# Single PSUM banks, load orders and sums of squares in a hybrid attention block

## The chip, the cores and the metric

One Trainium2 chip, one of its cores. The metric is the device time of one execution in microseconds; the time of a kernel is the median of its runs. A profile comes from one execution that the hardware profiler recorded. Five engines work beside each other: TensorE (PE, matrix products), VectorE (DVE), ScalarE (ACT), GpSimd (POOL) and SyncE (SP). SP, ACT and POOL issue DMAs. Each engine takes its instructions strictly in order.

## The reference

One layer on a sequence of 1024 rows and 2048 columns, all in float32:

```python
hn = rmsnorm(h, norm_mix_g[i])
proj = hn @ w_in[i]                         # q, k, v, gate of two head groups
sb_out = stick_breaking_attention(...)      # 8 heads of 128
df_out = differential_attention(...)        # 8 heads, two softmaxes each
mixed = concatenate([sb_out * silu(sb_g), df_out * silu(df_g)])
h = h + mixed @ w_out[i]                    # the output projection
gate = sigmoid(rmsnorm(h, norm_ple_g[i]) @ w_ple_gate[i])
h = h + gate * (p[i] @ w_ple_proj[i])       # the embedding product
return rmsnorm(h, norm_final_g)
```

What follows is about the rows from the output projection on, and about the PSUM banks of the stage that makes values and gates.

## The kernel before

Everything is held transposed: 16 blocks of 128 columns of the model (the partitions) by two halves of 512 rows (the free size). One such block, 128x512 float32, is the unit of nearly every load and every vector instruction.

**Products.** A float32 product is made of three fast ones: operand and weight are each split into a rounded high part and a low rest, and high x high, high x low and low x high are added in PSUM. The high part is a copy on ScalarE, the low part a subtraction on VectorE. On top of that the kernel multiplies 2x2 block matrices with seven products instead of eight. The seven have the names A11, A12, S1, S2, S3, S4 and A22; weights are turned into differences first (`T1` to `T4` on VectorE, line 759, for the value stage and the projection; `second_diffs`, lines 1720 to 1724, for the gate, whose transformed weights S3 and A22 are stored in `tw_d` and loaded again by `last_load`, line 1702).

**Stages, in the order of time.** First values and gates (class `Seven`, object `gv`), then q, k and attention by heads, then the output projection (`Seven`, object `op`: first the products A11 and A12 of phase 0 for all blocks, then the loop over phase and block), then the gate stage: p1, p2 and gate1 for the products A11 and A12, p6, p5 and p3 for S2, S1 and S4, and the last stage for S3 and A22 (`begin` and the loop behind it) with the final norm.

**Order.** The orders of TensorE, VectorE and ScalarE are those of the text of the program. SP's and GpSimd's orders are made by a planner that simulates the program; `tc.issue_after(x)` puts an instruction behind x on its queue. `op.step()` is called after each product: it makes the high part (`whigh`, lines 792 and 794) and the low part (`wlow`, 806 and 808) of one weight that is needed some products later, then runs what is due in `op.soon`, then up to two or three operand splits out of `op.xq` (`split`, lines 679 to 687). So a ScalarE that waits for one late load holds every later cast back.

**Banks.** PSUM has eight banks of 128x512 float32. Pool `pp` has two tags, acc and t, with two banks each. Pool `pz` has two tiles of two banks each, for attention's scores; the other stages take one tile for a pair of sums b and c, or half of one.

**Squares.** After each block of the projection's second phase (32 blocks) and after each block of one half in the gate stage (16), ScalarE squares it and a GpSimd DMA adds it into a tile in DRAM, `sq_d`, two tiles for each of three sums. Before each norm the two tiles are loaded (`load_sums`) and one product with a matrix of ones for each adds over the partitions (`norm`, line 1931).

Of the kernel before, what the change touches and what calls it, by code (L numbers as in the profile page):

```python
# [70 lines left out]
def _body(ctx, nc, tc, ap):  # L71
# [552 lines left out]
    with tc.tile_pool(name="at", bufs=2) as at, tc.tile_pool(name="pz", bufs=2, space=PSUM) as pz:  # L624
# [363 lines left out]
        for _ in range(2):  # L988
            z = pz.tile([P, 2, HALF], F32, name="paz", tag="z")
            aa += [z[:, 0, :], z[:, 1, :]]  # L990
# [216 lines left out]
        for ph in range(2):  # L1207
            for u in range(2 * H):
# [117 lines left out]
        sq_d = dram.tile([3, 2, P, HALF], F32, name="sq_d", tag="sq_d")  # L1326
        SUMS = "S1", "S2", "S3", "S4"

        def load_operand(ph, nm, i, eng=nc.sync):
# [4 lines left out]
            if src is None:  # L1334
# [40 lines left out]
        nsq = [0, 0, 0, 0]  # L1375

        def add_squares(k, s):


            n = nsq[k]  # L1380
            nsq[k] += 1
            G.dma_start(sq_d[k, n % 2], s, **(dict(accum_op=ALU.add) if n > 1 else {}))
# [86 lines left out]

        for half in (1, 0):  # L1470
# [200 lines left out]
        op.ticks = True  # L1671
        gneg = ev.tile([P, NK], F32, name="gneg", tag="zm", bufs=1)
# [25 lines left out]
        def last_load(u, nm):  # L1698
            if u < 8:
                w = wp.tile([P, 2, 4 * P], F32, name="wraw", tag="wraw", bufs=2)  # L1700
                raws[u, nm] = [w[:, ks, :] for ks in range(2)]
                nc.sync.dma_start(w, tw_d[u, int(nm == "A22")])
# [4 lines left out]
        def second_hook(u, ks):  # L1707
            if (u, ks) == (6, 1):
# [9 lines left out]
        def second_diffs(u, ks):  # L1718
# [6 lines left out]
            if 1 <= u < 7:  # L1725
                for b in (12, 11, 22, 21):
                    second_load(u + 1, ks, b)
# [17 lines left out]
        for u in range(8):  # L1745
            for nm in ("S2", "S1", "S4"):
# [72 lines left out]
        def plew_load(u, c):  # L1819
            if u < 8:  # L1820
                pws[u, c] = ev.tile([P, 2, P], F32, name="pw", tag="sm", bufs=5)
                nc.sync.dma_start(pws[u, c], ap["w_pp"][u][:, :, c, :])
# [17 lines left out]
        for ph in range(2):  # L1840
            for u in range(8):
# [16 lines left out]
                elif ph == 1 and u == 7:  # L1858
                    b = pz.tile([P, 2, HALF], F32, name="pbc", tag="z")[:, 0, :]
                    c = None  # L1860
                else:
                    bc = pz.tile([P, 2, HALF], F32, name="pbc", tag="z")
                    b, c = bc[:, 0, :], bc[:, 1, :]
# [27 lines left out]
                if ph:  # L1891
                    V.tensor_tensor(u3, u3, r[0, u + 8], op=ALU.add)
                    if u == 7:
                        c = pz.tile([P, 2, HALF], F32, name="pbc", tag="z")[:, 1, :]
# [14 lines left out]
        gate_loads("A12", 4)  # L1909

# [15 lines left out]
        def norm(tiles):  # L1926

            out = tiles[0]
            ps = pp.tile([P, HALF], F32, name="ssps", tag="t")
            for i, t in enumerate(tiles):  # L1930
                T.matmul(ps, ones, t, start=i == 0, stop=i == len(tiles) - 1)
# [13 lines left out]

        def load_sums(half, tags):
            r = []
            for i, (pool, tag, n) in enumerate(tags):
                r.append(pool.tile([P, HALF], F32, name="sums", tag=tag, bufs=n))
                op.loaded = nc.sync.dma_start(r[i], sq_d[half, i])  # L1950
            return r
# [9 lines left out]
        def gating1(u, c, o, z):  # L1961
# [5 lines left out]
            def squared():  # L1967
                t = hc.pop(u + 8 * c)
                A.activation(o, t, AF.Square)
                A.dma_start(h_d[1, u + 8 * c], t)  # L1970
                add_squares(1, o)
# [6 lines left out]
        def p1(u):  # L1978
            if u % 4 > 1:
                pa[u] = pz.tile([P, 2, HALF], F32, name="paz", tag="z")[:, 0, :]  # L1980
# [19 lines left out]

        p1(0)
        p1(1)
        p1(2)
        op.calm = False
        embedding_load(1, "f")
        sums2 = load_sums(2, ((ev, "rstd1", 1), (ev, "ssq", 1)))
        p2(0)
        p2(1)
        norm(sums2)
        ssh[1] = sums2[0]  # L2010
        embedding(1)
        plew_load(0, 0)
        plew_load(1, 0)
# [3 lines left out]
        plew(0, 0)  # L2017
# [28 lines left out]
        def p6(u):  # L2046
# [8 lines left out]
            parts2[u] = pz.tile([P, 2, HALF], F32, name="pc", tag="z")[:, 0, :], w  # L2055
# [20 lines left out]
        for u in range(8):  # L2076
            p6(u + 1)
            plew_load(u + 2, 1)
            load_hc(u + 9)
            if u == 5:  # L2080
                sums0 = load_sums(0, ((ev, "rstd0", 1), (ev, "ssq", 1)))
# [7 lines left out]
            if u < 7:  # L2089
                plew(u + 1, 1)  # L2090
                p5(u + 1)
            if u == 6:
                norm(sums0)
                ssh[0] = sums0[0]
# [5 lines left out]
        def load_h(u):  # L2100
            if u < 8:
                hpair[u] = at.tile([P, 2, HALF], F32, name="h0", tag=HP[u], bufs=BUFS.get(HP[u], 2))
                nc.sync.dma_start(hpair[u], h_d[0].rearrange("(a k) p t -> k p a t", a=2)[u])

        def load_q(u):

            r = []
            for i in range(2):
                r.append(xp.tile([P, HALF], F32, name="qt", tag=f"x{'hl'[i]}{KT[4 + u % 4]}"))
                nc.sync.dma_start(r[i], q_d[u, i])  # L2110
# [5 lines left out]
        for u in range(4):  # L2116
            load_h(u)
        qs = {u: load_q(u) for u in range(3)}
# [14 lines left out]
        def final1(ch, u_):  # L2133
            t = ftile()
            nc.sync.dma_start(t, h_d[1, ch])

            def fn():
                V.scalar_tensor_tensor(t, t, gvec[:, 2, ch:ch + 1], sums1[0], op0=ALU.mult, op1=ALU.mult)
# [261 lines left out]
```

## Time and profile before

| | us |
|---|---|
| median of 3 runs (2388.27 to 2389.63) | 2388.85 |
| the profiled execution | 2393.9 |
| its span, first to last instruction | 2392.1 |
| TensorE busy | 2332.3 |
| VectorE busy | 1781.2 |
| ScalarE busy | 1189.3 |
| GpSimd busy | 334.3 |

The span is what the profile sees; the execution lasts 1.8 us longer. A row of waits reads: the engine, the tile and line that waited, what it waited for, the microseconds in total, how often, the longest one. A row of a group reads: line, engine, operation, output and inputs, shapes and count, then busy time, mean nanoseconds of one, the idle time of the engine before them and what ended it. L1897 is line 1897 of the kernel before.

### The profile page before, as it was taken

Reading aid. Unit: us, or ns where it says so; the run is one execution under the profiler, and the core shown is the slowest. Engines: PE = TensorE matmul, PEld = TensorE weight load, DVE = VectorE, ACT = ScalarE, POOL = GpSimd, SP = SyncE. Lnnn points to the kernel's source line nnn. Section 1 sums busy time; section 2 is a strip of 40 time slices with the busy share of each in tenths; the row PEclk is TensorE's granted clock in tenths of the full one; section 3 lists DMA queues with packets and bytes.
Section 4 is the critical chain, followed back from the end, with each engine's and each line's share of the span. In section 5 each row is a group of like instructions: output and inputs, shape, how many; then the busy total and the mean of one; then the engine's idle time right before and its main releaser. Section 6 shows DMA issues by size and latency. Waiting matters only on the chain.

```text
span 2392.1 us, 32521 instructions
## 1 busy us (share of the span) xinstructions
PE 2332.3 (97%) x11102; PEld 1936.5 (81%) x11102; DVE 1781.2 (74%) x3107; ACT 1189.3 (50%) x2213; POOL 334.3 (14%) x497
## 2 busy tenths in 40 slices
PE   9999999999999999999999999999999999999997
PEld 7878878888788877887888888888878777778776
DVE  7489776666577787777888867768778886677687
ACT  6334243333366675445677764545634334533453
POOL 1211112323200000000011101101111231011000
PEclk9999999999999999999999999999999999999998
DMA  7798589999977788777656666668888899998955
GB/s 253 244 345 285 162 242 286 287 280 273 294 248 253 242 276 279 258 252 249 208 169 199 179 211 206 196 197 256 208 205 228 255 265 293 294 330 280 317 189 179
DMA packets 257510, 590.46 MB, mean 247 GB/s; under 512 B 29056, under 2 KB 41344, under 8 KB 257344
## 3 DMA queue, kind: packets, MB, share of 16 engines
q1 hardware_dynamic: 178384, 395.15, 48.8%
q0 software_dynamic: 59664, 158.10, 26.0%
q10 hardware_dynamic: 19296, 35.14, 4.3%
q8 instruction: 87, 1.43, 0.3%
q14 instruction: 79, 0.65, 0.1%
HBM read 374.37 MB, written 222.30 MB: 249 GB/s over the span
## 4 chain that ended last, share of the span: by engine, by line
PE 72%; DVE 11%; DMA 8%; ACT 7%; issue 2%; SPq 0%; ACTq 0%; DVEq 0%
PE acc L262 7%; PE acc L264 7%; PE acc L263 7%; PE pbc L703 6%; PE pbc L705 6%; PE pbc L704 6%; PE pa L705 2%; PE pa L704 2%; PE pa L703 2%; PE tp L481 2%; DMA wraw<-w_gate 1%; DMA wraw<-w_out 1%; PE pb L1918 1%; PE pb L704 1%; PE pb L705 1%
## 5 line engine op out<-in xcount | busy, mean ns | idle before, releaser
L794 ACT CAST wpr<-T 128x512 fp32r<-128x512 f32 x208 | 125.5, 620 | 442.9 <-DVE T L759 359.4
L262 PE MATMUL acc<-xh,whi 128*128 128x512 f32 x768 | 315.1, 410 | 0.0
L264 PE MATMUL acc<-xh,wlo 128*128 128x512 f32 x768 | 302.3, 394 | 1.1 <-DMA wlo<-wlo_d 1.1
L263 PE MATMUL acc<-xl,whi 128*128 128x512 f32 x768 | 301.0, 392 | 0.0
L264 PEld LDWEIGHTS acc<-xh,wlo 128*128 128x128 f32 x768 | 144.4, 188 | 35.0 <-DMA wlo<-wlo_d 2.3
L263 PEld LDWEIGHTS acc<-xl,whi 128*128 128x128 f32 x768 | 145.5, 189 | 24.0
L262 PEld LDWEIGHTS acc<-xh,whi 128*128 128x128 f32 x768 | 145.0, 189 | 23.8 <-DVE qk L1549 0.4
L794 ACT CAST wpr<-wraw 128x512 fp32r<-128x512 f32 x144 | 88.3, 616 | 148.3 <-DMA wraw<-w_gate 36.8
L808 DVE TENSOR_TENSOR wpr<-T,wpr 128x512 fp32r<-128x512 f32 x208 | 142.8, 686 | 13.1 <-ACT wpr L794 9.2
L927 POOL DMA_DIRECT2D vg_d<-hc x120 | 86.8, 724 | 344.1 <-DVE hc L1169 206.7
L808 DVE TENSOR_TENSOR wpr<-wraw,wpr 128x512 fp32r<-128x512 f32 x144 | 97.9, 686 | 38.6 <-ACT wpr L794 38.5
L504 DVE TENSOR_TENSOR awl<-tp,awh 128x256 fp32r<-128x256 f32 (+1 forms) x160 | 92.5, 578 | 43.0 <-ACT awh L499 42.2
L499 ACT CAST awh<-tp 128x256 fp32r<-128x256 f32 (+1 forms) x160 | 80.6, 503 | 82.6 <-PE tp L481 76.4
L322 DVE CUSTOM_DVE_ANT_0 z<-z,masks 128x512 f32<-128x512 f32 (+7 forms) x128 | 97.1, 769 | 22.9 <-PE z L342 13.8
L703 PE MATMUL pbc<-cS,wpr 128*128 128x512 f32 x288 | 112.2, 389 | 0.8 <-DVE u L1225 0.8
L705 PE MATMUL pbc<-cS,wpr 128*128 128x512 f32 x288 | 112.1, 389 | 0.0
L704 PE MATMUL pbc<-cS,wpr 128*128 128x512 f32 x288 | 112.0, 389 | 0.0
L374 DVE TENSOR_TENSOR_SCAN st<-pt 128x511 f32<-128x511 f32 (+3 forms) x64 | 86.7, 1354 | 27.5 <-ACT pt L367 27.0
L367 ACT ACTIVATE pt<-z 128x512 f32<-128x512 f32 (+3 forms) x64 | 41.8, 653 | 76.9 <-DVE z L350 74.9
L529 PE MATMUL av<-awl,v 128*128 128x256 f32 x256 | 73.5, 287 | 2.0 <-DVE awl L504 2.0
L527 PE MATMUL av<-awh,v 128*128 128x256 f32 x256 | 72.0, 281 | 0.7 <-ACT awh L499 0.7
L528 PE MATMUL av<-awh,v 128*128 128x256 f32 x256 | 72.2, 282 | 0.0
(570 smaller groups left out, 6831.8 us busy)
## 6 DMA issues: line engine op xcount, KB each, us to landing
wlo<-wlo_d SPq DMA_DIRECT2D x94, 512.0 KB, 5.1
whi<-whi_d SPq DMA_DIRECT2D x74, 512.0 KB, 4.0
wraw<-w_vg SPq DMA_DIRECT2D x130, 256.0 KB, 4.6
vg_d<-hc POOLq DMA_DIRECT2D x120, 256.0 KB, 5.5
wraw<-w_in SPq DMA_DIRECT2D x54, 512.0 KB, 5.3
wraw<-w_gate SPq DMA_DIRECT2D x92, 256.0 KB, 5.4
wraw<-w_out SPq DMA_DIRECT2D x72, 256.0 KB, 4.8
wlo_d<-wlo SPq DMA_DIRECT2D x34, 512.0 KB, 3.4
```

The lines of the kernel that those rows point to most:

```text
L262: T.matmul(acc[c], hi[:, k2, kh, c, :], xh, start=first, stop=False)
L263: T.matmul(acc[c], hi[:, k2, kh, c, :], xl, start=False, stop=False)
L264: T.matmul(acc[c], lo[:, k2, kh, c, :], xh, start=False, stop=last)
L322: V.tensor_tensor_reduce(z, z, mwide[:, 0:n], -DF_SCALE, 3.0e38, ALU.add, ALU.min, mx)
L374: V.tensor_tensor_scan(st[:, off + 1:nkey], pt[:, off:nkey - 1], pt[:, off:nkey - 1], initial=1.0, op0=ALU.mult, op1=ALU.bypass)
L504: V.tensor_tensor(wl[:, o, :], tp[:, o, :], wh[:, o, :].bitcast(F32), op=ALU.subtract)
L703: T.matmul(o, wh[:, w], xh, start=start and k == 0, stop=False, skip_group_check=True)
L704: T.matmul(o, wh[:, w], xl, start=False, stop=False, skip_group_check=True)
L705: T.matmul(o, wl[:, w], xh, start=False, stop=k == 3, skip_group_check=True)
L794: A.copy(t[:, 0], src)
L808: V.tensor_tensor(t[:, 1], src, t[:, 0].bitcast(F32), op=ALU.subtract)
L927: G.dma_start(vg_d[hf, blk, u], o, **(dict(accum_op=ALU.add) if ph else {}))
```

## The change

Five things change together.

- Banks: outside attention the four banks of `pz` become four single tiles, `single(name)`. The pool is closed and opened anew around attention.
- Sums of squares: `sq_d` is gone. For the projection's 32 blocks ScalarE squares into one scratch tile (the mask's memory, `spare32`) and GpSimd adds it into a total in SBUF. For the 16 blocks of the gate stage VectorE adds into that scratch tile. A norm takes one tile.
- Places and times of the gate's operands (`GPLACE`, `NEXT`, `GNEXT`): A11, A12, S1, S4 and A22 take other buffers; three of A12's last four are loaded earlier.
- The gate's order: S2 and S1 of blocks 0 and 1 come before S4 of both, in the weights and in the products (`p5(1)` before `p3(0)`); one weight block of block 2 is loaded in S4's hook.
- Loads that follow others: the embedding's weights, `h`, `q` and the final loads are issued behind `op.loaded`, which the loads of transformed weights now set; fewer of them are loaded in advance. The embedding's first weights are cast earlier.

```diff
+    with tc.tile_pool(name="at", bufs=2) as at, ExitStack() as banks:
+        def singles(name):
+            banks.close()
+            pool = banks.enter_context(tc.tile_pool(name=name, bufs=4, space=PSUM))
+            return lambda nm: pool.tile([P, HALF], F32, name=nm, tag="z")
+
+        single = singles("pv")
...
-                    bc = pz.tile([P, 2, HALF], F32, name="pbc", tag="z")
-                    b, c = bc[:, 0, :], bc[:, 1, :]
+                    b, c = single("pbc"), single("pbc")
...
-        GPLACE = {"A11": XP[0:4] + FREE1, "A12": XP[4:12], "S2": FREE2 + [("at", t) for t in ("k", "k2", "v2", "v")],
-                  "S1": XP[12:16] + FREE1, "S4": XP[4:12], "S3": XP[0:4] + FREE2, "A22": XP[12:16] + XP[8:12]}
-
-        NEXT = {"A11": [("A11", 0)], "S3": [("A11", 4, 3)], "S1": [("A11", 7, 1), ("A12", 0)]}
+        GPLACE = {"A11": XP[0:4] + XP[8:12], "A12": XP[4:8] + FREE1, "S2": FREE2 + [("at", t) for t in ("k", "k2", "v2", "v")],
+                  "S1": XP[12:16] + XP[8:12], "S4": XP[4:8] + FREE1, "S3": XP[0:4] + FREE2, "A22": XP[12:16] + XP[8:12]}
+
+        NEXT = {"A11": [("A11", 0)], "S2": [("A11", 4, 3)], "S3": [("A11", 7, 1)], "S1": [("A12", 4, 3), ("A12", 0)]}
         GNEXT = {("A11", 1): [("S1", 4)], ("A12", 0): [("S4", 0)], ("A12", 1): [("S4", 4)],
-                 ("S2", 1): [("S3", 4)], ("S1", 1): [("A22", 0)], ("S4", 1): [("A22", 4)]}
+                 ("S2", 1): [("S3", 4)], ("S1", 1): [("A22", 0), ("A22", 4)]}
...
-        def add_squares(k, s):
-            n = nsq[k]
-            nsq[k] += 1
-            G.dma_start(sq_d[k, n % 2], s, **(dict(accum_op=ALU.add) if n > 1 else {}))
+        spare32 = masks.bitcast(F32)[:, 0:HALF]
+        totals = {}
 
         def row_squares(hf, o):
-            n = nsq[3]
-            nsq[3] += 1
-            t = ev.tile([P, HALF], F32, name="rsq", tag=f"rstd{n % 2}", bufs=1)
-            A.activation(t, o, AF.Square)
-            add_squares(2 * hf, t)
+            if hf not in totals:
+                totals[hf] = ev.tile([P, HALF], F32, name="total", tag=f"rstd{hf}", bufs=1)
+                A.activation(totals[hf], o, AF.Square)
+            else:
+                A.activation(spare32, o, AF.Square)
+                G.tensor_tensor(totals[hf], totals[hf], spare32, op=ALU.add)
...
         def second_hook(u, ks):
+            if u == 0:
+                second_load(2, ks, 22)
...
-        for u in range(8):
-            for nm in ("S2", "S1", "S4"):
+        for u, nms in [(0, ("S2", "S1")), (1, ("S2", "S1")), (0, ("S4",)), (1, ("S4",))] + [(u, ("S2", "S1", "S4")) for u in range(2, 8)]:
+            for nm in nms:
...
-                nc.sync.dma_start(pws[u, c], ap["w_pp"][u][:, :, c, :])
+                with tc.issue_after(op.loaded.ins):
+                    nc.sync.dma_start(pws[u, c], ap["w_pp"][u][:, :, c, :])
...
-        gate_loads("A12", 4)
+        gate_loads("A12", 7, 1)
...
             def squared():
                 t = hc.pop(u + 8 * c)
-                A.activation(o, t, AF.Square)
+                if u + c == 0:
+                    A.activation(spare32, t, AF.Square)
+                else:
+                    A.activation(o, t, AF.Square)
+                    V.tensor_tensor(spare32, spare32, o, op=ALU.add)
                 A.dma_start(h_d[1, u + 8 * c], t)
-                add_squares(1, o)
...
         p5(0)
         for u in range(8):
             p6(u + 1)
+            if u == 0:
+                p5(1)
...
-        for u in range(4):
+        for u in range(2):
             load_h(u)
-        qs = {u: load_q(u) for u in range(3)}
+        qs = {u: load_q(u) for u in range(2)}
```

`last_load` keeps its DMA as `op.loaded`; `load_h`, `load_q` and `final1` issue theirs behind it.

More of the change, by code (lines that the diff above doesn't have):

```diff
@@ L987, in _body @@
         aa = [pp.tile([P, HALF], F32, name="pa", tag=t, bufs=2) for t in ("acc", "acc", "t", "t")]
-        for _ in range(2):
-            z = pz.tile([P, 2, HALF], F32, name="paz", tag="z")
-            aa += [z[:, 0, :], z[:, 1, :]]
+        aa += [single("paz") for _ in range(4)]
         def outer(n):
@@ L1701, in last_load @@
                 raws[u, nm] = [w[:, ks, :] for ks in range(2)]
-                nc.sync.dma_start(w, tw_d[u, int(nm == "A22")])
+                op.loaded = nc.sync.dma_start(w, tw_d[u, int(nm == "A22")])
         def second_load(u, ks, b):
@@ L1893, in _body @@
                     if u == 7:
-                        c = pz.tile([P, 2, HALF], F32, name="pbc", tag="z")[:, 1, :]
+                        c = single("pbc")
                         prod(u, ph, "S1", c, True)
@@ L1924, in gprod, with norm @@
                 op.step()
-        def norm(tiles):
-            out = tiles[0]
+        def norm(out):
             ps = pp.tile([P, HALF], F32, name="ssps", tag="t")
-            for i, t in enumerate(tiles):
-                T.matmul(ps, ones, t, start=i == 0, stop=i == len(tiles) - 1)
+            T.matmul(ps, ones, out, start=True, stop=True)
             def roots():
@@ L2016, in _body @@
         load_hc(1)
-        plew(0, 0)
         gate_loads("S2", 0, eng=A)
@@ L2109, in load_q @@
                 r.append(xp.tile([P, HALF], F32, name="qt", tag=f"x{'hl'[i]}{KT[4 + u % 4]}"))
-                nc.sync.dma_start(r[i], q_d[u, i])
+                with tc.issue_after(op.loaded.ins):
+                    nc.sync.dma_start(r[i], q_d[u, i])
             return r
@@ L2214, in _body @@
         W = {(u, nm, ks): op.wq.pop((u, "g" + nm, ks)) for u in (6, 7) for nm in ("S3", "A22") for ks in range(2)}
-        z = {u: pz.tile([P, 2, HALF], F32, name="ple", tag="z") for u in (6, 7)}
+        z = {(u, c): single("ple") for u in (6, 7) for c in range(2)}
         Q = HALF // 2
```

74 lines of the change are left out of this document (33 added, 41 removed).

## The prediction

> **What bounds the kernel now.** I read the page's first part, then TensorE's busy time by stretches, then the waits of TensorE, then the queues around each wait.
>
> ```profile
> span 2392.1 us, 32521 instructions
> PE 2332.3 (97%) x11102; PEld 1936.5 (81%) x11102; DVE 1781.2 (74%) x3107; ACT 1189.3 (50%) x2213; POOL 334.3 (14%) x497
> ```
>
> TensorE sets the time; no edit here takes a product away, so gain must come out of its stalls. Busy time understates them (a matmul lasts 0.39 us but the next starts sooner), so I count matmuls in stretches of one shape (columns: stretch and length; busy us and count of TensorE, its weight loads, DVE, ACT, POOL; granted clock; DMA share; GB/s):
>
> ```profile
> 1750.00:1836.00 86.00, 86.00 (x382) 71.19 (x381) 64.50 (x102) 26.57 (x47) 16.27 (x19) 1.00 0.86 214
> 1733.80:1746.00 12.20, 7.72 (x26) 5.59 (x25) 7.67 (x12) 3.33 (x6) 0.85 (x1) 0.86 0.57 144
> 1855.00:1978.00 123.00, 120.63 (x527) 98.17 (x526) 99.59 (x154) 45.54 (x82) 34.02 (x50) 1.00 0.93 261
> 1997.60:2028.70 31.10, 29.52 (x125) 23.01 (x124) 18.13 (x28) 16.30 (x28) 3.72 (x5) 1.00 0.89 275
> 2028.70:2051.00 22.30, 19.24 (x82) 14.82 (x81) 12.50 (x21) 10.96 (x18) 0.00 (x0) 1.00 0.88 301
> 2100.00:2134.00 34.00, 29.48 (x114) 23.14 (x113) 27.26 (x46) 15.20 (x28) 4.28 (x6) 0.90 1.00 339
> 2246.00:2257.00 11.00, 9.76 (x40) 7.13 (x39) 8.53 (x14) 8.24 (x14) 1.45 (x2) 1.00 1.03 375
> 2257.00:2287.00 30.00, 27.99 (x123) 22.54 (x122) 23.82 (x41) 15.76 (x29) 0.87 (x1) 1.00 0.93 314
> 2287.00:2343.00 56.00, 56.00 (x245) 45.70 (x244) 45.79 (x76) 30.77 (x54) 0.00 (x0) 1.00 0.58 196
> ...
> 60.00:630.00 570.00, 564.47 (x2476) 465.15 (x2475) 398.45 (x597) 211.85 (x347) 135.58 (x209) 1.00 0.88 270
> ```
>
> The first row is a stretch without a stall. A window also counts the matmul cut by its edge, some 1.7 of them, so the pace is 86 / 380.3 = 0.227 us, and a product of 12 takes 2.72 us. Length less 0.227 x (count less 1.7) is what a window lost, to about 0.3 us in a short one; the four passes of a norm (three windows) are taken out of the count and stay in the loss. In order: 6.7, 3.8, 4.0, 4.1, 8.5, 3.2, 2.5 and 1.7 us, 34.5 from the output projection on; and some 8 us in the value and gate stage, the last row. The granted clock of 0.86 and 0.90 in two of them says that a long stall is paid again in slow matmuls after it. The eighth window has no stall, only a norm, so a norm's four passes cost 1.7 us.
>
> Whom TensorE waited for:
>
> ```profile
> PE pbc L703 <- ACT wpr L794: 4.5, 1, 4.5
> PE z L1836 <- ACT pwhl L1828: 3.6, 2, 2.2
> PE pbc L703 <- DVE hc L1247: 3.5, 2, 2.5
> ...
> PE pbc L703 <- DVE hq L1897: 2.3, 3, 0.9
> ...
> PE pb L1920 <- DVE wpr L808: 1.9, 1, 1.9
> ...
> PE pc L1918 <- DVE hc L2061: 1.7, 2, 1.2
> ...
> PE pa L1918 <- DVE o L1996: 1.6, 1, 1.6
> ...
> PE pbc L703 <- DVE hc L1169: 1.3, 2, 0.8
> ```
>
> **The change part by part.**
>
> *Banks.* A product that adds into half of a two-bank tile waits for readers of both halves. In the projection, A22 adds into b, which L1890 reads; TensorE waits for L1897, which reads c:
>
> ```profile
> 1895.53 0.69 DVE L1890 TENSOR_TENSOR u<-pbc,s 128x512 f32<-128x512 f32 x1
> ...
> 1896.98 0.69 DVE L1897 TENSOR_TENSOR hq<-pbc,u 128x512 f32<-128x512 f32 x1
> ```
>
> With a bank of its own, b is free 1.45 us earlier (1896.98 less 1895.53), more than the longest wait, 0.9: the 3.8 us of the window from 1855 go if DVE is no later than now. In the value stage the same edit drops one instruction of about 0.7 us from both L1247 waits and all of the two L1169 waits: 0.7 + 0.7 + 1.3 = 2.7 us of the 8; nothing if DVE falls as far back again, 5 if the slow clock after the 2.5 us wait goes too. I take 2.7. Reopening the pools adds no instruction; if it adds a wait, that shows at the projection's first product into a new bank. For L1996, p1(4) no longer takes the bank that gate1(0) still reads.
>
> *Order of loads at the projection's start.* DVE stood 4.72 us for a block of w_out, while five loads of w_pp, not needed for 300 us, went out on SP's queue around it:
>
> ```profile
> 1721.09 1.28 SPq L1822 DMA_DIRECT2D pw<-w_pp  x2
> ...
> 1723.07 0.55 SPq L1822 DMA_DIRECT2D pw<-w_pp  x1
> 1723.71 0.78 SPq L750 DMA_DIRECT2D wraw<-w_out  x1
> 1724.53 1.25 SPq L1822 DMA_DIRECT2D pw<-w_pp  x2
> pw<-w_pp SPq DMA_DIRECT2D x32, 128.0 KB, 4.7
> 1736.66 0.69 DVE L759 TENSOR_TENSOR T<-wraw 128x512 f32<-128x512 f32 x1 [4.72 <-DMA wraw<-w_out]
> ```
>
> Held behind the gate's first operands, they leave. Five loads of a median 4.7 us are about what DVE lacked. I take 6.5 of 6.7; nothing if GpSimd's three adds into comb_d in the same microseconds are the cause.
>
> *Squares: 48 DMAs that add up in DRAM, and six loads of the sums, go.*
>
> ```profile
> L1382 POOL DMA_DIRECT2D sq_d<-rsq x32: 542/868/1212, 1854.7 to 2010.5; - x32
> L1382 POOL DMA_DIRECT2D sq_d<-o x16: 552/879/929, 2058.1 to 2275.0; - x16
> L934 POOL MEMSET wide<- x1: 526/526/526, 0.9 to 0.9; 128x512 f32 x1
> q0 software_dynamic: 7056, 17.04, 46.8%
> L1965 DVE TENSOR_TENSOR hc<-hc,o 128x512 f32<-128x512 f32 x16 | 11.1, 692 | 0.6
> L1969 ACT ACTIVATE o<-hc 128x512 f32<-128x512 f32 x16 | 10.1, 630 | 8.8 <-DVE hc L1965 8.8
> ```
>
> The q0 row (packets, MB, share of the DMA engines) is of 1850 to 2015: 17.04 MB are 65 GpSimd DMAs of 128x512 f32 (0.262 MB); they held 46.8% of 165 us, 1.19 us each, so the 32 there free 38 us of DMA time, 23% of a stretch whose share is 0.89 to 0.93, and the 16 later ones 19 us. In their place come 30 GpSimd adds of 128x512, and 15 DVE adds in the gate stage. No row has a GpSimd add. Below stands the memset of that shape, 0.53 us for one stream; two inputs and an output, one after another, give 1.6. I take the middle, 1.1. GpSimd has room (34 of 123 us), and with one scratch tile ScalarE's next square waits for the add: at most one square in a product's 2.72 us, and 0.63 (L1969's squares) + 1.6 = 2.2 fits; behind it on ScalarE would stand the next weight cast.
>
> What can cost is DVE. If an add keeps DVE standing for g us, all of its length or a part, 24 fall into the window from 1855 (30 x 123 / 156), where DVE is idle 23.4 us: 0.98 us each, and beyond it DVE sets the pace. Below that an add in the burst before L1890 still eats the banks' 1.45. I leave 1.8 of the 3.8 us; the ends are 3.8 gained and, at 1.6 us, 24 x 0.62 = 15 lost.
>
> The Trainium skill speaks against this edit: SBUF — State Buffer, "Who interferes with whom", lets a VectorE instruction with two SBUF inputs and a GpSimd one that reads SBUF exclude each other for a whole instruction, and GPSIMD Engine Reference, "Elementwise — side-by-side cycle accounting", has 4497 ns for an add of 2048 elements, an estimate of 1.12 us for 512. By both the sum would be some 5 us smaller (24 x 0.14, and the 1.8). No row here shows it: there is no GpSimd add in this trace.
>
> *Norms.* One sum tile instead of two halves 1.7 us, three times. At 2247 TensorE waits for L2061 right behind the norm, so that one is worth nothing: 2 x 0.85 = 1.7.
>
> *Start of the gate.*
>
> ```profile
> 2019.82 0.72 ACT L681 ACTIVATE cgA12h<-cgA12l,gvec 128x512 fp32r<-128x512 f32 x1 [2.74 <-DMA cgA12l<-h_d]
> 2041.18 0.40 ACT L1828 CAST pwhl<-pw 128x256 fp32r<-128x256 f32 x1 [0.40 <-ACT s L1985]
> L794 ACT CAST wpr<-wraw 128x512 fp32r<-128x512 f32 x96 | 58.7, 614 | 103.3 <-DMA wraw<-w_gate 36.8 <-DMA wraw<-tw_d 34.0 <-DMA wraw<-w_out 23.9
> ```
>
> Three of the last four A12 loads now go out one product earlier, and 23% less stands before the fourth: 2.3 us (4.0 less the norm), none if it still lands late. The cast at 2041.18 moves ahead of the norm's work, and the bank of L1996 is free: I take 3.5 of 4.1.
>
> *Order of S2, S1, S4 (window 2100 to 2134).* S2 of block 1 is made two weights earlier, and S4's first use comes one product pair (5.4 us) later, past its late loads. The first half of the loss, the cast for the eighth embedding product, waits for S1's operands, helped only by lighter traffic. 5.5 of 8.5; ends 2 and 8.5.
>
> *Last stage.*
>
> ```profile
> 2247.01 2.74 SPq L2103 DMA_DIRECT2D h<-h_d  x4
> ...
> 2252.60 3.54 SPq L2110 DMA_DIRECT2D qt<-q_d  x3
> qt<-q_d SPq DMA_DIRECT2D x16, 256.0 KB, 5.0
> ```
>
> The h and q loads go ahead of the transformed weights that ScalarE waits for (34.0 us above); now they follow those. 2.0 of 2.5, ends 0 and 2.5. The loss at 2246 stays.
>
> *New waits.* Each DVE add is 0.69 us plus a wait of up to 0.63 for its square, behind it the next low weight half; 15 make 20 us where DVE is about 80% busy (27.26 of 34), so mostly covered. At L808 and L2061 TensorE waited for DVE three times; 3 x 0.69 = 2. The q loads come with one block less lead: 2 more. Ends 0 and 9.
>
> Sum: 2.7 + 6.5 + 1.8 + 1.7 + 2.3 + 3.5 + 5.5 + 2.0 = 26.0, less 4 = 22.0. The profiled execution took 2393.9 us (span 2392.1 and 1.8 around it), 5 above the median: 2371.9 against it, 2366.9 against the median of 2388.85.
>
> **The rivals.**
> 1. *Adds stop DVE* (place: 1853 to 2010). For: DVE is the busiest engine after TensorE there, and most of its instructions read two SBUF tiles. Against: 23.4 us of idle DVE. Mild, g = 1.2: 24 x 0.22 = 5.3 and the 1.8 more, 2374. Slower than before only from g = 0.98 + 20.2 / 24 = 1.82 us on, with nothing left of the 1.8; at 2.2 us it is 24 x 1.22 less 20.2 = 9.1 over, 2398. That lies beyond my upper bound of 1.6.
> 2. *Loads stay the bound*: the waits for w_gate come back once TensorE is earlier. Half of the gate's 13.3 us is lost: 2373.6. For: shares of 0.88 to 1.00; against: 57 us of DMA time less.
> 3. *Held loads come too late* in the last stage. A q load lands in 5.0 us, and S3 covers 5.4; 2 us late in six blocks is 10 us: 2377.
> 4. *Everything goes* but the 2246 loss and the untouched part of the value stage: 2.7 + 6.7 + 3.8 + 1.7 + 2.3 + 4.1 + 8.5 + 2.5 = 32.3, 2356.5.
>
> **How the numbers follow.** Forecast 45% (2362 to 2372); mild form of 1 13%, its slow form 6%; 2 14%; 3 10%; 4 12%. About 0.2%, 4.8 us, can be told from no change. The range, 2356 to 2384, reaches from 4 to 2 and 3 together. Slower 0.08 (the slow form and a late load in the tail), within 0.2% 0.07 (two of the rivals at once), faster 0.85.
>
> **What would show it.** Right: no DVE wait for w_out near 1731 and a clock of 1.00 there; no TensorE wait for L1897's successor; a GpSimd add near 1.1 us; DMA share near 0.70 from 1850 to 2000; norms of two passes; no waits for the embedding's weights at 2041. Wrong: DVE instructions of over 0.7 us beside adds, ScalarE waiting for GpSimd, waits for q or h loads after 2260, or the w_out wait still there.

## The result and the profile after

| | before | after |
|---|---|---|
| median, us (4 runs each) | 2388.56 (2388.14 to 2389.63) | 2366.27 (2361.72 to 2369.79) |
| profiled execution, us | 2393.9 | 2369.79 |
| TensorE busy, us | 2332.3 | 2321.1 |
| VectorE busy, us | 1781.2 | 1809.0 |

The ratio is 0.9908, with a 95% interval from 0.9893 to 0.9924. 2366.9 was forecast. The total agrees to 0.6 us; several of its terms do not, and their errors cancel, so that agreement is luck. The two profiled executions differ by 24.1 us.

The first lines of the page of the changed kernel:

```profile
span 2368.0 us, 32422 instructions
PE 2321.1 (98%) x11096; PEld 1932.0 (82%) x11096; DVE 1809.0 (76%) x3122; ACT 1189.4 (50%) x2213; POOL 336.0 (14%) x479
```

TensorE's busy time by stretches, columns as in the prediction (stretch and length; busy us and count of TensorE, weight loads, VectorE, ScalarE, GpSimd; clock; DMA share; GB/s):

```profile
1724.00:1737.00 13.00, 11.16 (x40) 8.12 (x39) 10.31 (x17) 4.47 (x8) 1.28 (x2) 0.87 0.67 156
1847.00:1970.00 123.00, 120.89 (x528) 98.50 (x527) 114.90 (x152) 44.60 (x79) 45.88 (x48) 1.00 0.62 209
1970.00:1993.70 23.70, 21.71 (x89) 17.45 (x89) 21.88 (x29) 15.28 (x26) 11.50 (x12) 0.93 0.82 282
1993.70:2021.00 27.30, 27.30 (x122) 22.62 (x121) 18.93 (x28) 13.55 (x24) 2.18 (x3) 1.00 0.82 280
2021.00:2043.00 22.00, 22.00 (x97) 17.87 (x96) 13.10 (x22) 12.68 (x21) 0.00 (x0) 1.00 0.75 245
2092.00:2126.00 34.00, 34.00 (x151) 28.16 (x150) 32.40 (x54) 15.14 (x29) 2.18 (x4) 1.00 0.90 313
2222.00:2233.00 11.00, 10.95 (x47) 8.47 (x46) 10.11 (x17) 8.94 (x14) 0.54 (x1) 1.00 0.86 283
2233.00:2262.00 29.00, 29.00 (x129) 24.02 (x129) 25.36 (x43) 17.20 (x32) 0.00 (x0) 1.00 0.71 246
...
60.00:630.00 570.00, 565.62 (x2487) 465.95 (x2485) 399.32 (x602) 213.05 (x351) 135.61 (x209) 1.00 0.88 271
```

With the prediction's measure (length less 0.2267 us for each matmul but 1.7) the rows from 1993.70 on lost next to nothing beyond a norm's two passes: the gate's stalls are gone, all of them. The first three rows still lose 4.3, 3.7 and 3.9 us. There are two places: the stall near 1731 is still there, only shorter, and the projection's second phase, 1847 to 1993.7, now loses 7.6 us, where the same work before lost 3.8. It became slower. The rows of waits name what TensorE waited for:

```profile
PE pbc L709 <- DVE u L1893: 4.1, 6, 2.0
...
PE pbc L709 <- DVE u L1248: 3.1, 3, 1.7
...
PE pbc L709 <- ACT wpr L800: 1.8, 1, 1.8
...
PE pbq L2228 <- DVE qt L2235: 1.3, 1, 1.3
PE pb L709 <- DVE u L1248: 1.3, 2, 0.9
```

The first is the second phase: L1893 is the read of b that L1890 was before. The edit to the banks did what it says, TensorE now waits for the reader of b and no longer for that of c; but that reader is late. The fourth is new and lies in the tail.

Since matmuls come in the same order in all these kernels, each stage can be timed from the start of its first matmul to that of the next stage's. This table is worked out so, in us, with the least time that the stage's matmuls take at 0.2267 us (norms not counted):

```
                        v and g  attention  projection 1  projection 2  gate A11,A12  S2,S1,S4  S3,A22   tail
matmuls x 0.2267                               108.8         152.3          97.9        141.5     81.6
before                   666.65   1056.51      116.75        156.28        109.82       149.55    85.93   30.54
after                    663.77   1054.54      113.99        159.83         98.82       142.60    82.51   32.15
gain                       2.9       2.0          2.8          -3.6          11.0          7.0      3.4    -1.6
```

From the gate's start up to the tail, profiles of kernels with the same code in a stage agree within 0.5 us, with one exception (143.7 for S2, S1, S4 in e10). The first two columns do not: 659.9 to 664.5 for values and gates over the kernels that have the new banks there, 662.4 in e6, which has the old ones, and some 5 us for attention, which nothing here touches. Also the first phase varies, 111.1 to 114.0 with the same code. The second phase takes 159.83 us here and 158.23 in e7, which has the same code and the same 2.0 us wait in it; the difference is the granted clock behind that wait, 0.93 here (third row above) and 1.00 in e7:

```profile
1968.80:1992.50 23.70, 21.71 (x96) 17.66 (x95) 23.48 (x31) 15.27 (x26) 12.18 (x13) 1.00 0.82 277
```

So a run's time varies by several us, and the experiments are read by stages.

### The profile page after: what moved, and what is told of

Its sections match the earlier page's. It is cut to its first block, busy times and chain, and to the rows that moved or that the text cites. A ratio compares the mean times of both kernels' runs of the same rounds, so it can differ in the third digit from the quotient of the medians.

```text
span 2368.0 us, 32422 instructions
## 1 busy us (share of the span) xinstructions
PE 2321.1 (98%) x11096; PEld 1932.0 (82%) x11096; DVE 1809.0 (76%) x3122; ACT 1189.4 (50%) x2213; POOL 336.0 (14%) x479
## 4 chain that ended last, share of the span: by engine, by line
PE 66%; DVE 13%; issue 8%; ACT 7%; DMA 4%; POOL 1%; SPq 0%; DVEq 0%; POOLq 0%; ACTq 0%
PE acc L264 7%; PE acc L262 6%; PE acc L263 6%; PE pbc L709 5%; PE pbc L711 5%; PE pbc L710 5%; PE tp L481 2%; PE pa L711 2%; PE pa L710 2%; PE pa L709 2%; PE pc L1920 1%; PE pb L1922 1%; PE pc L1922 1%; PE pb L1920 1%; PE pb L1921 1%
## 5 line engine op out<-in xcount | busy, mean ns | idle before, releaser
L263 PEld LDWEIGHTS acc<-xl,whi 128*128 128x128 f32 x768 | 145.4, 189 | 24.1
L814 DVE TENSOR_TENSOR wpr<-T,wpr 128x512 fp32r<-128x512 f32 x208 | 149.0, 716 | 12.8 <-ACT wpr L800 8.9
L814 DVE TENSOR_TENSOR wpr<-wraw,wpr 128x512 fp32r<-128x512 f32 x144 | 97.5, 684 | 23.2 <-ACT wpr L800 23.2
```

The source lines that it names most:

```text
L263: T.matmul(acc[c], hi[:, k2, kh, c, :], xl, start=False, stop=False)
L814: V.tensor_tensor(t[:, 1], src, t[:, 0].bitcast(F32), op=ALU.subtract)
```

## Experiments

### What the GpSimd adds cost

Of the 30 adds 28 stop a VectorE instruction. Two spots of the changed kernel, by the timeline of VectorE and then that of GpSimd (start, length, engine, line):

```profile
1872.92 0.68 DVE L1794 TENSOR_TENSOR hc<-pbc,s 128x512 f32<-128x512 f32 x1
1873.53 1.22 DVE L765 TENSOR_TENSOR T<-wraw,T 128x512 f32<-128x512 f32 x1
...
1885.66 1.82 DVE L1781 SCALAR_TENSOR_TENSOR hc<-hc,gneg,hq 128x512 f32<-128x512 f32 x1
1887.41 0.68 DVE L814 TENSOR_TENSOR wpr<-T,wpr 128x512 fp32r<-128x512 f32 x1
1888.01 0.68 DVE L1893 TENSOR_TENSOR u<-pbc,s 128x512 f32<-128x512 f32 x1
```

```profile
1872.90 1.29 POOL L1386 TENSOR_TENSOR total<-total,masks 128x512 f32<-128x512 f32 x1 [1.68 <-ACT masks L1385]
...
1876.02 1.80 POOL L1386 TENSOR_TENSOR total<-total,masks 128x512 f32<-128x512 f32 x1 [1.32 <-ACT masks L1385]
...
1885.64 1.29 POOL L1386 TENSOR_TENSOR total<-total,masks 128x512 f32<-128x512 f32 x1 [1.73 <-ACT masks L1385]
```

At 1885.64 the add begins; L1781, which begins 0.02 us behind it, lasts 1.82 us instead of 0.75: it stands until about the add's end. At 1872.90 the instruction beside the add is L1794, which reads one of its inputs from PSUM, and it keeps its 0.68; the next, L765, reads two tiles in SBUF and is stopped for the rest of the add. Groups of VectorE's instructions from 1847 to 1970 (count, then busy us and mean ns) show it over the phase, L1781 stopped each time and L814 in part:

```profile
L814 DVE TENSOR_TENSOR wpr<-T,wpr 128x512 fp32r<-128x512 f32 x25 | 22.6, 904 | 0.9 <-ACT wpr L800 0.2
L1781 DVE SCALAR_TENSOR_TENSOR hc<-hc,gneg,hq 128x512 f32<-128x512 f32 x6 | 11.0, 1826 | 0.2
```

In the phase's last block two operand splits of the gate are hit (L693, 2.45 and 2.42 us for two of 0.74 each) ahead of L1893, VectorE's timeline again:

```profile
1979.75 2.45 DVE L693 SCALAR_TENSOR_TENSOR cgA11l<-cgA11l,gvec,cgA11h 128x512 fp32r<-128x512 f32 x2
...
1983.32 2.42 DVE L693 SCALAR_TENSOR_TENSOR cgA11l<-cgA11l,gvec,cgA11h 128x512 fp32r<-128x512 f32 x2
1985.67 0.68 DVE L1893 TENSOR_TENSOR u<-pbc,s 128x512 f32<-128x512 f32 x1
```

From 1847 to 1970 VectorE was busy 114.9 us with 152 instructions, before 99.6 with 154: some 16.6 us for the 23 adds there, 0.72 each. This is what the Trainium skill says in SBUF — State Buffer, "Who interferes with whom": VectorE with two inputs in SBUF and a GpSimd instruction that reads SBUF share a port, whoever comes first holds it for the whole instruction, and a VectorE instruction with at most one SBUF input, outside its 2-port modes, goes free. The trace agrees: 1.82 against 0.75 us for the instruction that comes second, 0.68 for the PSUM reader, and 1.80 against 1.29 for the add at 1876.02, which begins 0.04 us behind an instruction of VectorE with two tiles in SBUF (L1872). In one case, an L1781 that begins 0.03 us ahead of an add, VectorE is stopped although its record starts first.

Six kernels then measured whether the adds are why TensorE waits.

**e1**: the adds on VectorE.

```diff
-                G.tensor_tensor(totals[hf], totals[hf], spare32, op=ALU.add)
+                V.tensor_tensor(totals[hf], totals[hf], spare32, op=ALU.add)
```

> The 30 adds of the projection's squares run on VectorE instead of GpSimd; the rest is the changed kernel. Theory A (a GpSimd add stops one VectorE instruction, which then lasts 1.2 to 1.8 us instead of 0.69): from 1847 to 1970 of the changed kernel VectorE is busy 114.9 us with 152 instructions, before 99.6 with 154, so the adds cost it some 16.6 us, 0.69 each for 24. An add on VectorE itself is 0.69 long, so the time stays within 4 us of the changed kernel (2362 to 2370), and no VectorE instruction there is longer than 0.75 us. Theory B (a GpSimd add is close to free, and the waits for L1893 have another cause): moving the adds puts 16.6 us more on VectorE, 99.6 + 16.6 + 16.6 would not fit into 123, and the time goes up by 8 us or more.

Measured: 2364.53 us (2361.88 to 2371.09), second phase 155.62 us, against 159.83. Theory A. 30 instructions more on VectorE cost it no more than 30 on GpSimd did, since those had stopped it for as long. The wait in the last block stays (1.9 us), but the clock stays at 1.00 behind it, so 1.6 of the 4.2 us between the two phases are not the adds' engine.

**e2**: the adds left out (the line above removed).

> The 30 GpSimd adds are left out: ScalarE still squares, but a total holds the square of the first block of its half alone, so the norms are wrong. It measures what the adds cost TensorE. From 1847 to 1993.7 of the changed kernel TensorE lost 7.7 us (length less 0.2267 us for each matmul), six waits for L1893 and slow matmuls behind them; the kernel before lost 3.8 in the same work. Theory A (the adds cause the waits): 0 to 1.5 us lost there, 2358 to 2361. Theory B (VectorE's own order causes them): the waits stay, 2365 to 2368.

Measured: 2361.68 us (2359.10 to 2364.12), second phase 152.32 us, which is the bare matmul time; no wait for the reader of b is left. Here L1780 and L1892 are what L1781 and L1893 were:

```profile
1885.05 0.75 DVE L1780 SCALAR_TENSOR_TENSOR hc<-hc,gneg,hq 128x512 f32<-128x512 f32 x1
1885.72 0.68 DVE L814 TENSOR_TENSOR wpr<-T,wpr 128x512 fp32r<-128x512 f32 x1
1886.45 0.69 DVE L1892 TENSOR_TENSOR u<-pbc,s 128x512 f32<-128x512 f32 x1
```

So the adds are the whole cause: 7.5 us of TensorE's time, 5.9 in a run like that of e7 in which the clock doesn't fall. The median is 0.7 above the range that was expected.

**e3**: the 32 blocks' squares added in DRAM as before, all else as changed.

```diff
-                G.tensor_tensor(totals[hf], totals[hf], spare32, op=ALU.add)
+            G.dma_start(sq_d[hf, m % 2], t, **(dict(accum_op=ALU.add) if m > 1 else {}))
...
+        sums2 = load_sums(1, ((ev, "rstd1", 1), (ev, "ssq", 1)))
...
-        norm(totals[1])
+        norm(sums2)
```

> The 32 blocks' squares are added by GpSimd DMAs in DRAM as in the kernel before, and loaded as two halves before two norms; banks, places, orders, held loads and the gate stage's VectorE adds stay as changed. Theory A: the waits for L1893 in the projection go (7.7 us to under 1.5). Two norms get two passes more each, 1.7 us. What the gate's start does tells two further theories apart. C (lighter traffic freed the gate's start): with 32 DMAs more before and at its start (1.19 us of all DMA engines each, 38 us) 4 to 8 us of waits come back between the first gate product and the embedding's first products: 2364 to 2370. D (the new places and orders freed it): none come back, 2360 to 2363.

Measured: 2370.18 us (2365.67 to 2372.66), an interval of the ratio to before from 0.9897 to 0.9934. The second phase takes 152.32 us, though the DMA engines are busy 0.98 of its time from 1850 to 1973; traffic alone stops neither VectorE nor TensorE there. With the sums still in DRAM the stage wins back all of the 4.0 us that it lost before. The single banks take the waits for L1897 away, but not all of the 4.0 is shown to be theirs: in e6, which has the old banks and only holds the loads of w_pp, the stage takes 154.71, 1.6 less than before. The gate's first stage takes 105.76 us instead of 98.82: 0.9 for the norm's passes and 6.1 in waits, in the rows of its waits:

```profile
PE z L1840 <- ACT pwhl L1832: 2.0, 2, 1.2
PE pa L1920 <- ACT s L1990: 1.6, 1, 1.6
```

Theory C, then: lighter traffic freed most of the gate's start, and the other edits the remaining 4.1 us (109.82 to 105.76). The held loads of w_pp alone bring this stage to 107.26 in e6, so new places, orders and banks are not shown to be worth more than some 1.5. The median lies 0.2 above the range for C. For S2, S1 and S4 the traffic made no difference beyond the norm (143.27 and 142.60).

**e4**: one square later.

```diff
-                    put(hq[:, 0, :], ph, 1, u)
+                    put(hq[:, 0, :], ph, 1, u, 2)
```

> One of four squares of the projection's second phase (that of A12's block) is made one product later, so that its add starts behind L1893 instead of stopping the instruction of 1.83 us ahead of it (L1781). Theory A: the five waits of 0.33 to 0.48 us for L1893 go with the slow matmuls behind them, 3.7 us, and the sixth of 2.0 becomes about 1: 2360 to 2363. Theory B: no difference, 2365 to 2368.

Measured: 2365.78 us (2364.13 to 2369.46), second phase 160.26 us. The edit missed. VectorE's timeline, then GpSimd's:

```profile
1885.34 0.75 DVE L1781 SCALAR_TENSOR_TENSOR hc<-hc,gneg,hq 128x512 f32<-128x512 f32 x1
1886.00 1.79 DVE L814 TENSOR_TENSOR wpr<-T,wpr 128x512 fp32r<-128x512 f32 x1
1887.71 0.68 DVE L1893 TENSOR_TENSOR u<-pbc,s 128x512 f32<-128x512 f32 x1
```

```profile
1885.83 1.40 POOL L1386 TENSOR_TENSOR total<-total,masks 128x512 f32<-128x512 f32 x1 [2.25 <-ACT masks L1385]
```

L1781 is free, as wanted, but the add comes only 0.5 us nearer to L1893 and stops L814, which also stands ahead of it. The square had moved by one cast on ScalarE, and ScalarE had been waiting 4.1 us for L765 before both casts: a product in the program's order was half a microsecond in time.

**e10**: the same idea with larger distances.

```diff
-                op.soon.append((op.slot + 1, partial(row_squares, hf, o)))
+                op.soon.append((op.slot + lag, partial(row_squares, hf, o)))
...
-                    put(hq[:, 0, :], ph, 1, u)
+                    put(hq[:, 0, :], ph, 1, u, 5 if u == 7 else 3)
...
-                put(o, ph, 0, u + 8)
+                put(o, ph, 0, u + 8, 4 if u == 7 else 2)
...
-            put(o, ph, hf, ch)
+            put(o, ph, hf, ch, 5 if ph == 1 and u > 5 else 1)
```

> GpSimd adds as in the changed kernel, but the squares that start them stand elsewhere: that of A12's block three products after it instead of one, that of S1 and S3's block two, those of the last six blocks four or five. No add then stops an instruction just ahead of L1893. If the place decides: the second phase's 672 matmuls take 152.3 to 154 us as in the proposal on VectorE, and the time is 2358 to 2361. If a GpSimd add is dearer than one on VectorE wherever it stands: 156 to 160, 2363 to 2367.

Measured: 2359.51 us (2358.30 to 2363.03), ratio to before 0.9890 (0.9874 to 0.9906), second phase 152.32 us. The same instructions on the same engines, and 7.5 us less in the stage (5.9 less than in e7). VectorE reaches L1893 unstopped, and the next add starts 4.7 us later:

```profile
1881.82 0.75 DVE L1781 SCALAR_TENSOR_TENSOR hc<-hc,gneg,hq 128x512 f32<-128x512 f32 x1
1882.49 0.68 DVE L814 TENSOR_TENSOR wpr<-T,wpr 128x512 fp32r<-128x512 f32 x1
1883.09 0.68 DVE L1893 TENSOR_TENSOR u<-pbc,s 128x512 f32<-128x512 f32 x1
```

```profile
1887.75 1.30 POOL L1386 TENSOR_TENSOR total<-total,masks 128x512 f32<-128x512 f32 x1 [1.49 <-ACT masks L1385]
```

So the adds need not leave GpSimd. Moved, they also stop VectorE for less in all: it is busy 137.1 us of this phase instead of 149.9. This run alone doesn't tell the place from that sum; e1 and e9 together do.

**e9**: the adds on VectorE, placed.

```diff
-                G.tensor_tensor(totals[hf], totals[hf], spare32, op=ALU.add)
+                op.soon.insert(0, (op.slot + 1, lambda: V.tensor_tensor(totals[hf], totals[hf], spare32, op=ALU.add)))
...
+            put(o, ph, hf, ch, 5 if ph == 1 and u > 5 else 1)
...
+                    put(hq[:, 0, :], ph, 1, u, 5 if u == 7 else 1)
...
+                put(o, ph, 0, u + 8, 4 if u == 7 else 1)
```

> A proposal: the 30 adds run on VectorE, each one product after its square so that VectorE doesn't wait for ScalarE, and the squares of the last six blocks are made four products later, behind L1893 of the last block. The second phase's 672 matmuls take 159.83 us in the changed kernel, 155.62 with the adds on VectorE at once, 152.3 without adds and without a stall. Theory A: 152.3 to 153.5, and 2358 to 2361 against about 2366. If it is VectorE's load of 0.69 us for each add that costs, not the place where it stands: 155 to 156, 2362 to 2365.

Measured: 2358.32 us (2356.01 to 2367.28), ratio to before 0.9884 (0.9866 to 0.9902), second phase 152.32 us. It is faster than both kernels, than the changed one by some 8 us between the medians and some 6 by the ratios. The interval of the ratio overlaps that of the changed kernel a little (0.9893 to 0.9924); the stage, 7.5 us shorter, leaves no doubt. VectorE is busy 143.0 us in this phase, in e1 with the same 30 adds 144.3, and e1 lost 3.3 us where this run lost nothing. With the work all but the same, the place of the add decides.

### What is left of the w_out stall

In the changed kernel VectorE still waits 2.05 us for a block of w_out, with no load of w_pp near it. What goes out ahead of that load, by the timelines of VectorE and GpSimd:

```profile
1729.14 0.69 DVE L765 TENSOR_TENSOR T<-wraw 128x512 f32<-128x512 f32 x1 [2.05 <-DMA wraw<-w_out]
```

```profile
1717.49 0.86 POOL L302 DMA_DIRECT2D comb_d<-sg  x1 [10.02 <-DVE sg L541]
1718.03 1.19 POOL L306 DMA_DIRECT2D comb_d<-sg  x1
1718.58 1.53 POOL L307 DMA_DIRECT2D comb_d<-sg  x1
1719.23 1.76 POOL L1394 DMA_DIRECT2D h_d<-hc  x1
```

These four add up in DRAM, 0.26 MB each. The load went out at 1721.14 and landed 7.9 us later.

**e5**: the three into `comb_d` issued later.

```diff
+        if hd == ORDER0[-1]:
+            return
         if second:
             G.dma_start(S1, t, accum_op=ALU.add)
...
+                if (ph, u) == (0, 2):
+                    x = ev.tile([P, HALF], F32, name="last", tag="xt", bufs=4)
+                    nc.sync.dma_start(x, mixed_d[0, ORDER0[-1]])
+                    for j in (0, 1, 3):
+                        G.dma_start(comb_d[1, j, 3], x, accum_op=ALU.add)
```

> GpSimd's three accumulating DMAs of the last head into comb_d, which go out at 1717.5 to 1718.6 in the changed kernel and are needed only in the second phase, are issued two units later from a copy loaded again. TensorE's time for the 480 products' matmuls of the projection's first phase (from its first product into pb to the first of the second phase) is 113.99 us in the changed kernel's profile, 116.75 before, and 480 x 0.2267 = 108.8 without a stall; VectorE waited 2.05 us for a block of w_out that took 7.9 us to land while those adds were under way. Theory E (these adds hold the block): 108.8 to 110, no wait of VectorE for w_out, 2360 to 2364. Theory F (the loads of w_pp were the whole cause and what is left has another): the wait stays, the stage keeps 111 to 114.

Measured: 2365.18 us (2362.31 to 2370.88), first phase 110.37 us. TensorE's wait for a late weight is gone and the clock stays at 1.00, in the same stretch of this kernel:

```profile
1721.00:1733.00 12.00, 11.96 (x50) 9.20 (x51) 11.16 (x20) 4.87 (x9) 4.34 (x5) 1.00 0.89 176
```

This is nearer to theory E, but not all of it came: the stage is 0.4 us above the range for E, and VectorE still waits for w_out, later, while the moved adds are under way (landing in 7.3 us in the median); TensorE does not wait there:

```profile
1736.14 0.70 DVE L767 TENSOR_TENSOR T<-wraw 128x512 f32<-128x512 f32 x1 [1.45 <-DMA wraw<-w_out]
```

The median is above the range that was expected, too; with a stage that gains 0.7 to 3.6 us and runs that vary by 8 it can't say more.

**e6**: the kernel before with the loads of w_pp held.

```diff
-                nc.sync.dma_start(pws[u, c], ap["w_pp"][u][:, :, c, :])
+                with tc.issue_after(op.loaded.ins):
+                    nc.sync.dma_start(pws[u, c], ap["w_pp"][u][:, :, c, :])
```

> The kernel before, in which only the loads of w_pp are issued behind op.loaded. The first phase takes 116.75 us before and 113.99 in the changed kernel's profile. Theory E: the adds into comb_d stay, so a part of the stall stays: 111 to 114.5, 2382 to 2387. Theory F: 109 to 110 and 2380 to 2382. If the held loads don't matter at all there: 116 to 117 and 2388.

Measured: 2382.53 us (2378.22 to 2388.97) against 2387.98 for the kernel before, ratio 0.9978 (0.9963 to 0.9993), first phase 112.34 us against 116.75. By these single profiles the w_pp loads were some two thirds of the stall (4.4 us, slow matmuls behind it included), the adds into `comb_d` the rest (2.0, from 112.34 to the 110.37 of e5). With a phase that varies by 2.9 us for the same code the split is rough. The held loads also shortened the two stages that follow, by 1.6 and 2.6 us (154.71 and 107.26).

**e11**: e5 and e9 together.

> Paced adds on VectorE and the last head's adds into comb_d later, together. First phase 110.4 us (111.8 with the first alone, 110.4 with the second alone), second phase 152.3: 1.4 us less than the paced adds alone, 2355 to 2359; the two don't touch each other.

Measured: 2359.87 us (2355.68 to 2362.39). The stages are as expected, 110.34 and 152.32, but the median is 0.9 above the expected range and no lower than that of e9: 1.4 us is less than the scatter of values, gates and attention in five runs.

### The gate's order and the held loads

**e7**: S4 of blocks 0 and 1 back in its old place; the weight block of block 2 that S4's hook had loaded goes back with it (not shown in the diff).

```diff
-        for u, nms in [(0, ("S2", "S1")), (1, ("S2", "S1")), (0, ("S4",)), (1, ("S4",))] + [(u, ("S2", "S1", "S4")) for u in range(2, 8)]:
+        for u, nms in [(u, ("S2", "S1", "S4")) for u in range(8)]:
...
-            if u == 0:
-                p5(1)
```

> The changed kernel with S4 of blocks 0 and 1 back in its old place (S2, S1, S4 block by block in weights and products, no earlier load of block 2's weight); everything else stays. The stage of S2, S1 and S4 takes 149.55 us before (1.7 of it the four passes of a norm), 142.60 in the changed kernel (0.9), 143.27 with the sums added in DRAM (1.7). If the order won the stage's gain: 147 to 149 and 2370 to 2373. If the lighter traffic and the held loads won it: 142.6 to 144 and 2365 to 2368.

Measured: 2371.35 us (2367.95 to 2372.03), the stage 147.59 us instead of 142.60. The order is worth 5.0 of the stage's 7.0 us, the norm 0.9; two waits come back:

```profile
PE pb L1919 <- DVE wpr L814: 2.4, 2, 1.7
PE pc L1917 <- DVE hc L2053: 1.7, 1, 1.7
```

**e8**: h and q loads not held (in the diff `if True` stands for the removed `issue_after`).

```diff
-                with tc.issue_after(op.loaded.ins):
+                if True:
                     nc.sync.dma_start(hpair[u], h_d[0].rearrange("(a k) p t -> k p a t", a=2)[u])
...
-                with tc.issue_after(op.loaded.ins):
+                if True:
                     nc.sync.dma_start(r[i], q_d[u, i])
```

> The changed kernel with the h and q loads of the last stage not held behind op.loaded; their lead of two blocks stays. The last stage (S3 and A22 of six blocks) takes 85.93 us before and 82.51 in the changed kernel (one norm's two passes, 0.9, are of that), the tail from its first quarter product on 30.54 and 32.15. Theory G (holding them lets the transformed weights land in time): 83.5 to 85 for the stage, the tail back at 30.5 to 31. Theory H (the shorter lead does both): 82.5 and 32 as in the changed kernel.

Measured: 2367.09 us (2365.86 to 2372.28), the stage of S3 and A22 85.04 us instead of 82.51, the tail 30.54 instead of 32.15. Theory G. The waits come back ahead of a block's S3:

```profile
PE pb L1920 <- ACT pwhl L1832: 1.5, 1, 1.5
```

Holding the loads gives 2.5 us in this stage. In other kernels with the same holds the tail took 30.7 to 32.1, so what they cost there, 0.2 to 1.6 us, depends on the run. Ahead of the changed kernel's tail no engine waits for h or q. ScalarE waits for blocks of w_pp and, behind them, of transformed weights (2.2 us), and VectorE 1.8 us behind ScalarE:

```profile
2317.54 0.41 ACT L1832 CAST pwhl<-pw 128x256 fp32r<-128x256 f32 x1 [3.42 <-DMA pw<-w_pp]
2319.33 0.41 ACT L1832 CAST pwhl<-pw 128x256 fp32r<-128x256 f32 x1 [1.39 <-DMA pw<-w_pp]
```

In e8 there is no such wait for w_pp, in e10 (tail 30.74) one of 1.9 us. That this is what the tail's time hangs on was not tried.

## Why the prediction was right and wrong

- *Single banks, values and gates* (2.7): the window from 60 to 630 gained 2.5 us. Of that 1.1 stands in every kernel with the edit (its last 577 matmuls take 130.6 us instead of 131.7, the L1169 waits); the rest lies within what this stage varies, and e6 with the old banks took less time for the whole stage (662.4) than this kernel did (663.8). "Nothing if DVE falls as far back again" came half true: TensorE now waits for the reader of b at L1248, 4.4 us in five waits.
- *w_out stall* (6.5): 2.8 in this profile, 4.2 to 5.6 in the others with the same first phase. The step that failed is taking 6.5 of 6.7 with "nothing if GpSimd's three adds into comb_d are the cause". It was no either-or: both delay the block. The slow clock came back with the rest of the stall, 0.87 against 0.86; in e7 and e8, where TensorE waited as long (1.8 and 1.9 us), it stayed at 1.00.
- *Banks of the projection, less what the adds eat* (1.8): -3.6, and this is the largest error; 1.6 of it is the slow clock that e7 doesn't have. The step that failed is the bound. It was taken from the pace of the whole phase: 0.98 us of stop for each add fit into VectorE's idle time, 0.72 came, and so nothing beyond "the banks' 1.45" was to be lost. But TensorE doesn't wait for VectorE's sum, it waits at L1893, one product's length (2.72 us) after S3, and there one stop of 1.07 us stands directly ahead; in the last block two of them, on operand splits, made a wait of 2.0. The first rival named the mechanism and its sign; its price was worked out from the sum and not from the place. The estimate beside the Trainium skill had spoken of some 5 us, and the total of this term was 5.4 short; since that estimate rests on the same sum over the phase, coming near is luck. That the add took 1.3 us in place of 1.1 is the smaller part: adds of 0.69 us on VectorE at the same places still lost 3.3 us (e1).
- *Traffic*: GpSimd's queue fell more than forecast (23% of the DMA engines' time). Its row for 1842 to 2007, about the stretch that 1850 to 2015 was before:

```profile
q0 software_dynamic: 2704, 8.65, 14.8%
```

  17.04 less 8.65 MB are the 32 DMAs, and 32.0% of 165 us are 53 us, some 1.65 each instead of the mean of 1.19. Either those into `sq_d` were dearer than the rest, or the rest became cheaper without them (those from hc to h_d landed in 2.4 us in the median instead of 4.5); the runs don't tell the two apart.
- *Start of the gate and embedding* (2.3 and 3.5, and a norm's 0.85): all 7.2 went (4.0 and 4.1 less the norm that is left). With the old traffic (e3) TensorE waits 1.6 us at the first A12 product, but not for a late A12 operand: it waits for ScalarE's copy of a bank (s, L1990), and ScalarE had waited 9.6 us for a block of w_gate. At the fourth operand it waits 0.3.
- *Order of S2, S1, S4* (5.5 of 8.5): all 8.5. The order gave 5.0 (e7). The first half, the eighth embedding product, was to be helped only by lighter traffic, and it was: e3 has 1.2 us of it back.
- *The norm and loss at 2246* ("worth nothing", "stays"): both went, 2.3 us. The wait for L2061 that was to follow the norm does not come; what freed VectorE there was not tried by itself.
- *Last stage* (2.0 and a norm): 3.4, of which 2.5 from the holds (e8).
- *New waits* (-4): the VectorE adds of the gate stage cost TensorE nothing that shows. What was put down to q loads with less lead did not come in the blocks, so neither did the third rival; the tail cost 1.6, and no wait for a q load stands ahead of it.
- Attention, where nothing was forecast, was 2.0 shorter in this profile; it varies by more.

In sum: -3.7 at w_out and -5.4 in the second phase against +3.6 in the windows of the gate's start and order, +2.3 at 2246, +2.4 from waits that did not come, +2.0 from attention and 0.8 from the other terms: 2.0 more than the 22.0 forecast, of 24.1 measured. Of the signs that were to show the prediction wrong two came, VectorE instructions of over 0.7 us beside adds and the w_out wait, though the sum is right.

## What to carry to other kernels

An instruction that moves to another engine can still take the first engine's time: ask what the two share, and price it at the one instruction that somebody waits for, not against the idle time of a whole stage. Where two engines stop each other, moving the cheap work by a few steps (e10) was worth as much as leaving it out (e2). When a load is late, list everything that is under way beside it before putting the delay down to one; taking away one of two causes shortened TensorE's stall, and only both removed it.

## What the runs showed of the hardware

- A GpSimd add of 128x512 float32 with two SBUF inputs takes 1.29 us alone; the group's mean is higher, since it is stopped as well when a VectorE instruction with two SBUF operands is under way (1.80 us at 1876.02):

```profile
L1386 POOL TENSOR_TENSOR total<-total,masks 128x512 f32<-128x512 f32 x30 | 42.6, 1419 | 33.2 <-ACT masks L1385 26.2 <-DMA hr<-h_d 6.7
```

- A VectorE instruction with one PSUM operand is not stopped beside it (0.68 us), one with two SBUF operands is (up to 1.87 us). The DMA engines at 0.98 of their time stopped neither TensorE nor VectorE (e3, where no VectorE instruction of the second phase is longer than 0.75 us).
- A wait of TensorE of 2.0 us can cost about twice its length, or hardly more than itself. The wait in the projection's last block stands in six kernels (1.9 to 2.0 us). In four of them (the changed one, e4, e5, e8) the granted clock is 0.93 in the 23.7 us around it, and 3.9 us are lost in the changed one; in two (e1, e7) it stays at 1.00, and e7 loses 2.3.
